# Softmax attention of a hybrid trunk on one core: scores transposed, heads in pairs, maxima ahead

## The chip, the cores and the metric

The kernel runs on one core of a Trainium2 chip. The metric is the device time of one execution in microseconds (us). Three runs of the kernel before took 1719.51, 1723.79 and 1723.97 us, median 1723.79.

## What is computed

Two trunk layers work on 512 latent tokens and, in the first layer, on 256 context tokens with the same weights. Each layer has a modulated norm, one input projection, three groups of heads side by side (mean pooling, gated linear attention, softmax attention), an output projection with a gated residual, and a squared-ReLU MLP. The change is in softmax attention: 8 query heads of 64 in four pairs, 2 key heads (pairs 0 and 1 use the first, 2 and 3 the second). Latent queries see 256 context keys and 512 latent keys in one softmax; context queries see the context keys.

```python
def gqa_attend(qb, k, v):
    s = jnp.einsum('bqhgd,bkhd->bhgqk', qb, k, preferred_element_type=jnp.float32) * HEAD_DIM ** -0.5
    p = jax.nn.softmax(s, axis=-1)
    return jnp.einsum('bhgqk,bkhd->bqhgd', p.astype(v.dtype), v)
...
    o_gl, _, _ = gla_bidir(*gla_features(gq, gk, gv, rf, rb, w_gate, b_gate), s_f, s_b)
...
    mix = jnp.concatenate([pool_mixer(p, w_pool, s_pool),
                           gla_output(o_gl, gg, g_gla, x.dtype),
                           latent_attention(ql, k_all, v_all)], axis=-1) @ w_out
```

In layer 1 the context's outputs aren't needed, only its keys and values, so only the latent queries are swept there.

## The kernel before, in words

Everything is tiled in 128 tokens: latent tiles 0 to 3, context tiles 4 and 5. Matrix products in reduced-precision fp32 keep fp32 precision by splitting each factor in a high and a low part: `wload` (L130 to L146) loads a weight tile into a buffer `raw`, ScalarE rounds it to `whi`, VectorE makes `wlo` as the difference, and a product is three passes (`passes`). `wp` has three buffers for `raw` and five each for "hi" and "lo"; `sp` has 33 slots of 128x768 for everything else in the attention stage. Accumulators are in PSUM: two of 1024 columns (`psA`), three of 512 (`psB`), one of 512 (`psC`).

The instructions of a layer are written by several generators, and the two strings `STEPS` say in what order their steps are written: g for gated linear attention, a for the other projections, m for modulation, t for softmax attention. Within softmax attention, `att_thread` (L1037) calls the pooling generator once per unit. A list scheduler then fixes the order on each engine when the program is built; each engine runs its own list in that order and waits by semaphores.

Softmax attention before. `k_stack` transposes the normalised keys and keeps, for each key head, `kh` (the high part on 64 partitions, twice) and `kl` (the low part, twice). `q_stack` (L1023) does the same for the queries of a pair of heads, with high and low part on top of each other in `qs`, so that one matmul over 128 rows with `kh` and one with `kl` give the exact score. A unit is two query tiles of a pair of heads, and there are 12 in layer 0 (eight latent, four context) and 8 in layer 1. For each of a unit's four score tiles [128 queries x 768 keys], TensorE does four matmuls (L974, L975), VectorE takes the row maximum (L977), and ScalarE does the exponential with the maximum as bias and the row sum as a by-product (L978). `value_part` of the unit before is written between them: per key tile four transposes of probabilities (`pT`, L992), an eviction by ScalarE or VectorE (`pe`, L996, L998), and two value matmuls for 256 queries each (`av`, L1001). At a unit's end the reciprocal sums are spread over 64 partitions by four small matmuls (`rb`, L1008) and multiplied in (L1014), the result is split in `mixh` (ScalarE, L1016) and `mixl` (GpSimd, L1017).

Around it run, on the same engines, the last part of gated linear attention: products `xq`, `xk` on VectorE and GpSimd (L699, L707), small diagonal blocks on TensorE (`att`, L722) copied by VectorE (`dg`, L735) and ScalarE (`AT`, L738), the output `o` (L756, L761), its norm (`ss` L771, `rg` L782), and pooling (`pool`, L920).

The output projection follows (`op`, L291): its weights `w_out` come through `raw` like all others.

## Time and profile before

| | us |
|---|---|
| median of three runs | 1723.79 (1719.51 to 1723.97) |
| span of the profiled execution | 1719.9 |
| TensorE busy | 1639.1 (95%) |
| VectorE busy | 866.9 (50%) |
| ScalarE busy | 656.9 (38%) |
| GpSimd busy | 480.3 (28%) |

The profile shows one execution; its own time is the span, 1719.9 us, and no time outside of it is shown with it. Busy time is the sum of an engine's instructions; TensorE's are pipelined, so the distance between starts says what a matmul costs, not its length. Attention of layer 0 lies between about 222 and 387 us, that of layer 1 between about 1179 and 1305 us. In a row of the timeline the columns are start, length, engine, line, operation, output from inputs, shape and count, with the idle time of the engine before it and what ended that in brackets. The groups give count, busy time, mean ns of one, and the engine's idle time before them.

### The profile page before, as it was taken

How to read it: one execution, taken by the hardware profiler on the slowest of the kernel's cores; microseconds unless marked ns; L12 is line 12 of the kernel's file. 1: busy time of each engine (PE TensorE's matmuls, PEld its weight loads, DVE VectorE, ACT ScalarE, POOL GpSimd, SP SyncE). 2: the span in 40 equal slices, each digit the busy share in tenths (PEclk: the TensorE clock that was granted, in tenths of full speed). 3: DMA queues.
4: the chain of work that ended last, by engine and by line, in shares of the span. 5: the costliest groups of instructions: out<-in, count | busy, mean ns of one | idle time of the engine just before them, and what ended most of it. 6: DMA issues, size and time to landing. Idle time of an engine off the chain costs nothing.

```text
span 1719.9 us, 28685 instructions
## 1 busy us (share of the span) xinstructions
PE 1639.1 (95%) x12059; PEld 1337.3 (78%) x12059; DVE 866.9 (50%) x1209; ACT 656.9 (38%) x1136; POOL 480.3 (28%) x514
## 2 busy tenths in 40 slices
...
GB/s 309 131 85 75 136 161 3 100 27 122 111 138 96 153 50 184 120 94 147 50 122 56 68 89 75 72 2 2 2 74 130 79 99 98 99 98 98 98 98 49
DMA packets 140256, 163.38 MB, mean 95 GB/s; under 512 B 9412, under 2 KB 116304, under 8 KB 140128
## 3 DMA queue, kind: packets, MB, share of 16 engines
...
## 4 chain that ended last, share of the span: by engine, by line
PE 85%; DVE 5%; POOL 3%; DMA 2%; ACT 2%; issue 2%; SPq 0%; ACTq 0%; POOLq 0%; DVEq 0%
PE dn L291 25%; PE up L272 19%; PE op L291 7%; PE tm L291 6%; PE up L274 5%; PE fm L272 4%; PE av L1001 3%; PE pT L992 2%; PE pm L175 2%; PE up L281 2%; PE fm L274 2%; DMA rawm<-in_w_mod_dram 1%; PE sc L974 1%; PE att L722 1%; PE sc L975 1%
## 5 line engine op out<-in xcount | busy, mean ns | idle before, releaser
L144 ACT ACTIVATE whi<-raw 128x1024 fp32r<-128x1024 f32 (+2 forms) x182 | 184.8, 1031 | 582.2 <-PE dn L291 310.3
L1131 POOL TENSOR_TENSOR X<-X,rtmp 128x512 f32<-128x512 f32 x158 | 218.0, 1384 | 660.9 <-DVE rtmp L1130 660.6
L68 DVE TENSOR_TENSOR wlo<-raw,whi 128x1024 fp32r<-128x1024 f32 (+2 forms) x182 | 225.5, 1247 | 279.0 <-ACT whi L144 273.7
L291 PE MATMUL dn<-whi,ah 128*128 128x512 f32 x640 | 249.8, 390 | 0.4 <-DVE rtmp L1130 0.4
L291 PE MATMUL dn<-whi,al 128*128 128x512 f32 x640 | 249.1, 389 | 0.0
L291 PE MATMUL dn<-wlo,ah 128*128 128x512 f32 x640 | 246.8, 389 | 0.0
L1130 DVE TENSOR_TENSOR rtmp<-dn,ga 128x512 f32<-128x512 f32 x160 | 109.2, 689 | 231.4 <-PE dn L291 229.8
L272 PE MATMUL up<-h2h,whi 128*128 128x512 f32 x464 | 183.8, 396 | 0.7 <-ACT relu L1173 0.7
L272 PE MATMUL up<-h2l,whi 128*128 128x512 f32 x464 | 182.5, 393 | 0.0
L272 PE MATMUL up<-h2h,wlo 128*128 128x512 f32 x464 | 182.5, 393 | 0.0
L291 PEld LDWEIGHTS dn<-whi,ah 128*128 128x128 f32 x640 | 120.1, 188 | 29.8 <-ACT whi L144 4.2
L291 PEld LDWEIGHTS dn<-wlo,ah 128*128 128x128 f32 x640 | 120.1, 188 | 25.0
L291 PEld LDWEIGHTS dn<-whi,al 128*128 128x128 f32 x640 | 120.1, 188 | 24.5
L272 PEld LDWEIGHTS up<-h2h,whi 128*128 128x128 f32 x464 | 87.1, 188 | 31.4 <-ACT relu L1173 7.6
L272 PEld LDWEIGHTS up<-h2l,whi 128*128 128x128 f32 x464 | 87.1, 188 | 21.1 <-issue 1.7
L291 PE MATMUL tm<-whi,hTh 128*128 128x256 f32 (+1 forms) x352 | 102.6, 292 | 0.0
L272 PEld LDWEIGHTS up<-h2h,wlo 128*128 128x128 f32 x464 | 87.1, 188 | 19.6
L291 PE MATMUL tm<-whi,hTl 128*128 128x256 f32 (+1 forms) x352 | 101.3, 288 | 0.0
L291 PE MATMUL tm<-wlo,hTh 128*128 128x256 f32 (+1 forms) x352 | 100.5, 287 | 0.0
L291 PE MATMUL op<-whi,mixh 128*128 128x256 f32 x320 | 91.2, 285 | 0.9 <-ACT whi L144 0.9
L291 PE MATMUL op<-wlo,mixh 128*128 128x256 f32 x320 | 90.2, 284 | 0.3 <-DVE wlo L68 0.3
L291 PE MATMUL op<-whi,mixl 128*128 128x256 f32 x320 | 90.5, 283 | 0.0
...
## 6 DMA issues: line engine op xcount, KB each, us to landing
...
```

Source lines behind the costliest of these rows:

```text
L68: V.tensor_tensor(lo, full, hi.bitcast(F32), ALU.subtract)
L144: A.activation(hi, raw, AF.Copy)
L175: T.matmul(pm[32 * j:32 * j + 32, :], sstat[:, k, :], raw[:, (j % 2) * 512:(j % 2) * 512 + 512], start=(k == 0), stop=(k == KT - 1), skip_ ...
L272: T.matmul(ps[:, 0:NL], a, b[:, 0:NL], start=st, stop=sp_)
L274: T.matmul(ps[:, NL:NT], a, b[:, NL:NT], start=st, stop=sp_)
L281: T.matmul(ps[:, cs], a, b[:, cs], start=(k == 0 and i == 0), stop=(k == nk - 1 and i == 2))
L291: T.matmul(ps, a[:, sl], bb, start=(k == 0 and i == 0), stop=(k == nk - 1 and i == 2))
L722: T.matmul(ps[g * bw:(g + 1) * bw, o0:o0 + bw], xk[rows, j0:j0 + bw], xq[rows, i0:i0 + bw], start=True, stop=True)
L992: T.transpose(pt_[:, i * 128:(i + 1) * 128], p_[:, ki * 128:(ki + 1) * 128], ident)
L1001: T.matmul(av_[64 * hh:64 * hh + 64, 0:256], vst, pe[:, hh * 256:hh * 256 + 256], start=(ki == 0), stop=(ki == len(kts) - 1))
L1130: V.tensor_tensor(tmp, ps, ga[0 if t < 4 else 1][:, sl], ALU.mult)
L1131: (V if b == NB - 1 and not both and t == 3 else G).tensor_tensor(X[t][:, sl], X[t][:, sl], tmp, ALU.add)
```

## The change

Scores are computed transposed: 128 keys on the partitions, the 512 latent queries of a head along the columns, the two heads of a pair side by side in 1024 columns. So the exponentials of a key tile (`p`, one 128x1024 instruction) can be used as the moving operand of the value matmuls (`av`, 64x512 per head) without being transposed, and the 416 transposes of probabilities with their evictions are gone.

The maximum of a query is then one value per column, and it goes in by the matmul: `qm` holds the queries' high part on 64 partitions and minus the maximum in a 65th row, and the 65th row of `kl` is ones, written by ScalarE instead of the second copy of the low part that GpSimd made. The maxima must be known before the first score of the pair. `max_part` takes them from separate products, [128 queries x keys] as before but for a latent pair 3 x 512 columns per latent tile (`mxc` for the context keys of both heads, with high and low part of the queries; `mx` per head for the latent keys, high part only), reduced by VectorE (L981, L984) and moved into the 65th row by a matmul with the identity (`mT`, L992) and two ScalarE copies of one row (L995).

The row sum no longer comes with the exponential. GpSimd adds key tiles 0 to 3 (`acc`, L1041, L1043), VectorE tiles 4 and 5 and the two halves (L1049, L1050), in buffers of the pool `raw`; a matmul with ones adds over the partitions (`sum`, L1010). `weigh` takes the reciprocal by ScalarE's logarithm and exponential and one correction step on VectorE (L1013 to L1017), then splits the result as before. `weigh` is put in a list and written two steps later. `max_part` of the next pair is written between the steps of this pair, one step each. The pooling generator is called at every fifth step. Other lines of the diff take out comments and shorten `STEPS`.

```diff
 STEPS = ("aggaamgmagagaaagaaaamgaaaaamagaaaagaaaaaagmgaaaagamggmggmgtt"
-         "mggtttmtttgttgtmgtggtttgtttgttmgtmtgttmgtt",
...
+         "ggttttgtgtgtggttgttgtgtgtgt",
...
+    identr = const.tile([128, 128], F32R, name="identr")
+    V.tensor_copy(identr, ident)
+
+    nmx = const.tile([128, 6, 33], F32R, name="nmx")
+    A.activation(nmx, ident[:, 0:1].unsqueeze(1).to_broadcast([128, 6, 33]), AF.Copy, scale=0.0)
...
-                G.tensor_copy(kl[64:128], kl[0:64].bitcast(F32))
+                A.activation(kl[64:65], ident[64:65, 64:65].to_broadcast([1, NT]), AF.Copy)
...
+        def max_part(hp):
             mix_new(4 + hp)
             pq = [psB("qT"), psB("qT")] if both else [psB("qT")]
             for t in live:
                 T.transpose(pq[t // 4][:, (t % 4) * 128:(t % 4 + 1) * 128], qview(t, hp), ident)
             for hh in range(2):
+                qs, qm = slot("qs", F32R), slot("qm", F32R)
+                hr, lr = slice(64 * hh, 64 * hh + 64), slice(64 - 64 * hh, 128 - 64 * hh)
                 for i, pq_ in enumerate(pq):
                     n0, n1 = (0, NL) if i == 0 else (NL, NT)
+                    src = pq_[hr, 0:n1 - n0]
+                    A.activation(qs[hr, n0:n1], src, AF.Copy)
+                    sub_lo(qs[lr, n0:n1], src, qs[hr, n0:n1])
+                G.tensor_copy(qm[0:64, 0:N_], qs[hr, 0:N_].bitcast(F32))
+                qst[2 * hp + hh] = (qs, qm)
+            yield
+            kh = kst[hp // 2][0]
+            parts = mp.tile([128, 2, 6, 2], F32, tag="mxp", name=nm("mxp"), bufs=1)
+            for t in live:
+                ts_ = slice(t * 128, (t + 1) * 128)
+                ps = psB("mxc")
+                for hh in range(2):
+                    T.matmul(ps[:, hh * NC:(hh + 1) * NC], qst[2 * hp + hh][0][:, ts_], kh[:, NL:NT], start=True, stop=True)
+                if t < 4:
+                    pl_ = [psB("mx"), psB("mx")]
+                    for hh in range(2):
+                        hr = slice(64 * hh, 64 * hh + 64)
+                        T.matmul(pl_[hh], qst[2 * hp + hh][0][hr, ts_], kh[hr, 0:NL], start=True, stop=True)
+                V.tensor_reduce(parts[:, 1, t], ps.rearrange("p (h k) -> p h k", h=2), AX.X, ALU.max, negate=True)
+                if t < 4:
+                    for hh in range(2):
+                        V.tensor_reduce(parts[:, 0, t, hh:hh + 1], pl_[hh], AX.X, ALU.max, negate=True)
+                yield
+            V.tensor_tensor(nmx[:, 0:4, 0:33:32], parts[:, 0, 0:4], parts[:, 1, 0:4], ALU.min)
+            if both:
+                V.tensor_copy(nmx[:, 4:6, 0:33:32], parts[:, 1, 4:6])
+            yield
+            ps = psA("mT")
+            for t in live:
+                T.matmul(ps[0:33, t * 128:(t + 1) * 128], nmx[:, t], identr, start=True, stop=True)
+            for hh in range(2):
+                r0 = 32 * hh
+                A.activation(qst[2 * hp + hh][1][64:65, 0:N_], ps[r0:r0 + 1, 0:N_], AF.Copy)
+            yield
+        def scores(ps, hp, hh, kt, q0, qn):
+            kh, kl = kst[hp // 2]
+            qs, qm = qst[2 * hp + hh]
+            ks = slice(kt * 128, (kt + 1) * 128)
+            T.matmul(ps, kh[:, ks], qs[:, q0:q0 + qn], start=True, stop=False)
+            T.matmul(ps, kl[0:65, ks], qm[0:65, q0:q0 + qn], start=False, stop=True)
+        def weigh(hp, f, acc, q0, n):
+            sm = psB("sum")[:, 0:n]
+            for hh in range(2):
+                T.matmul(sm[64 * hh:64 * hh + 64], one.to_broadcast([128, 64]), acc[hh], start=True, stop=True)
+            r, u = slot("r", w=512)[:, 0:n], slot("u", w=512)[:, 0:n]
+            A.activation(r, sm, AF.Ln)
+            A.activation(r, r, AF.Exp, scale=-1.0)
+            V.scalar_tensor_tensor(u, r, -1.0, sm, ALU.mult, ALU.mult)
+            V.tensor_tensor(r, f, r, ALU.mult)
+            V.scalar_tensor_tensor(r, u, 2.0, r, ALU.add, ALU.mult)
+            mhi, mlo = mixT[4 + hp]
+            A.activation(mhi[:, q0:q0 + n], r, AF.Copy)
+            G.tensor_tensor(mlo[:, q0:q0 + n], r, mhi[:, q0:q0 + n].bitcast(F32), ALU.subtract)
+        def lat_part(hp):
+            av = psC("av")
+            P = []
+            def values(kt):
+                for hh in range(2):
+                    T.matmul(av[64 * hh:64 * hh + 64, :], vview(kt, hp // 2), P[kt][:, hh * 512:hh * 512 + 512],
+                             start=(kt == 0), stop=(kt == 5))
+            for kt in range(6):
+                s_ = psA("sT")
+                for hh in range(2):
+                    scores(s_[:, hh * 512:hh * 512 + 512], hp, hh, kt, 0, NL)
+                P.append(wp.tile([128, 1024], F32, tag="lo" if kt % 2 else "hi", name=nm("p")))
+                A.activation(P[kt], s_, AF.Exp)
+                if kt:
+                    values(kt - 1)
+                if kt == 1:
+                    acc = wp.tile([128, 1024], F32, tag="raw", name=nm("acc"), bufs=3)
+                    G.tensor_tensor(acc, P[0], P[1], ALU.add)
+                elif kt in (2, 3):
+                    G.tensor_tensor(acc, acc, P[kt], ALU.add)
+                yield
+            values(5)
+            acc2 = wp.tile([128, 1024], F32, tag="raw", name=nm("acc"), bufs=3)
+            f = slot("f", w=512)
+            A.activation(f, av, AF.Copy)
+            V.tensor_tensor(acc2, P[4], P[5], ALU.add)
+            V.tensor_tensor(acc, acc, acc2, ALU.add)
+            later.append([2, lambda: weigh(hp, f, [acc[:, 0:512], acc[:, 512:1024]], 0, NL)])
+            yield
+        def ctx_part(hp):
+            av = psC("avc")[:, 0:NC]
+            s_ = psA("sTc")
+            for hh in range(2):
+                for i in range(2):
+                    o = i * 512 + hh * NC
+                    scores(s_[:, o:o + NC], hp, hh, 4 + i, NL, NC)
+            p_ = wp.tile([128, 1024], F32, tag="hi", name=nm("p"))
+            A.activation(p_, s_, AF.Exp)
+            yield
+            for i in range(2):
+                for hh in range(2):
+                    o = i * 512 + hh * NC
+                    T.matmul(av[64 * hh:64 * hh + 64, :], vview(4 + i, hp // 2), p_[:, o:o + NC],
+                             start=(i == 0), stop=(i == 1))
+            f = slot("f", w=512)[:, 0:NC]
+            A.activation(f, av, AF.Copy)
+            acc = slot("accx", w=512)
+            G.tensor_tensor(acc, p_[:, 0:512], p_[:, 512:1024], ALU.add)
+            later.append([2, lambda: weigh(hp, f, [acc[:, 0:NC], acc[:, NC:512]], NL, NC)])
+            yield
+        later = []
+        def tick():
+            for e in list(later):
+                e[0] -= 1
+                if e[0] == 0:
+                    later.remove(e)
+                    e[1]()
         def att_thread():
             k_stack()
             yield
+            yield from max_part(0)
+            n = 0
+            for hp in range(4):
+                nxt = max_part(hp + 1) if hp < 3 else iter(())
+                next(nxt, None)
+                for part in (lat_part(hp), ctx_part(hp) if both else iter(())):
+                    for _ in part:
+                        next(nxt, None)
+                        tick()
+                        n += 1
+                        if n % 5 == 3:
+                            next(pool_, None)
+                        yield
+                for _ in nxt:
+                    tick()
                     yield
             run(pool_)
+            while later:
+                tick()
```

The order on TensorE in layer 0, first inside pair 2 of the kernel before: `sc` are score tiles, `pT` and `av` belong to the unit before.

```order
L1001 MATMUL av_586_4005<-pe_593_4036,UV_185_1137 64x256 x2
L992 MATMUL pT_600_4072<-ident_86,p_558_3910 128x128
L992 MATMUL pT_600_4072<-ident_86,p_559_3911 128x128
L992 MATMUL pT_600_4072<-ident_86,p_560_3912 128x128
L992 MATMUL pT_600_4072<-ident_86,p_561_3913 128x128
L974 MATMUL sc_599_4065<-kh_350_2665,qs_490_3634 128x512
L975 MATMUL sc_599_4065<-kl_351_2666,qs_490_3634 128x512
L974 MATMUL sc_599_4065<-kh_350_2665,qs_490_3634 128x256
L975 MATMUL sc_599_4065<-kl_351_2666,qs_490_3634 128x256
L1001 MATMUL av_586_4005<-pe_595_4045,UV_185_1137 64x256 x2
L1008 MATMUL rb_602_4082<-ident_86,sm_556_3908 64x128 x4
L1001 MATMUL av_586_4005<-pe_598_4061,UV_185_1137 64x256 x2
```

The same engine now, from the end of pair 1's value matmuls on: `mxc` and `mx` are the products for pair 2's maxima, `pool` is pooling, `sum_496` sums pair 0's context part.

```order
L1028 MATMUL av_489_3625<-p_519_3730,UV_185_1141 64x512 x2
L1028 MATMUL av_489_3625<-p_522_3743,UV_185_1141 64x512 x2
L975 MATMUL mxc_493_3634<-kh_350_2669,qs_485_3611 128x256
L927 MATMUL pool_517_3719<-pm_291_2163,wpl_138_743 128x256
L975 MATMUL mxc_493_3634<-kh_350_2669,qs_487_3618 128x256
L980 MATMUL mx_494_3637<-kh_350_2669,qs_485_3611 128x512
L980 MATMUL mx_495_3638<-kh_350_2669,qs_487_3618 128x512
L1010 MATMUL sum_496_3644<-accx_480_3599,one_97 64x256 x2
L975 MATMUL mxc_502_3667<-kh_350_2669,qs_485_3611 128x256
L975 MATMUL mxc_502_3667<-kh_350_2669,qs_487_3618 128x256
L980 MATMUL mx_503_3670<-kh_350_2669,qs_485_3611 128x512
L980 MATMUL mx_504_3671<-kh_350_2669,qs_487_3618 128x512
```

Score tiles stood between the transposes and value matmuls of the unit before; now the products for the next pair's maxima stand behind the last value matmul of the pair.

VectorE in layer 0 before, in pair 2: `nmx` are row maxima, `qs` the low part of the next queries, `pe` evictions.

```order
L977 TENSOR_REDUCE nmx_557_3909<-sc_572_3964 128x1
L68 TENSOR_TENSOR qs_578_3987<-qT_575_3974,qs_578_3987 64x512
L977 TENSOR_REDUCE nmx_580_3993<-sc_585_3998 128x1
L68 TENSOR_TENSOR qs_578_3987<-qT_576_3975,qs_578_3987 64x256
L980 RECIPROCAL sm_556_3908<-sm_556_3908 128x4
L977 TENSOR_REDUCE nmx_580_3993<-sc_591_4024 128x1
L998 COPY pe_593_4036<-pT_592_4031 128x512
L977 TENSOR_REDUCE nmx_580_3993<-sc_596_4049 128x1
L998 COPY pe_601_4077<-pT_600_4072 128x512
L977 TENSOR_REDUCE nmx_580_3993<-sc_599_4065 128x1
```

VectorE now, at the end of pair 2's scores: `acc_581` adds the exponentials of its last two key tiles, `mxp` are the maxima of pair 3, `pm` is pooling.

```order
L68 TENSOR_TENSOR qs_544_3834<-qT_540_3819,qs_544_3834 64x512
L68 TENSOR_TENSOR qs_544_3834<-qT_541_3820,qs_544_3834 64x256
L1049 TENSOR_TENSOR acc_581_3977<-p_573_3938,p_579_3967 128x1024
L981 TENSOR_REDUCE mxp_549_3849<-mxc_550_3850 128x2
L984 TENSOR_REDUCE mxp_549_3849<-mx_551_3853 128x1
L984 TENSOR_REDUCE mxp_549_3849<-mx_552_3854 128x1
L920 SCALAR_TENSOR_TENSOR pm_296_2220<-pl_536_3802,invw_121,pl_535_3801 64x512
L920 SCALAR_TENSOR_TENSOR pm_296_2220<-pl_537_3803,invw_121,pl_535_3801 64x512
L981 TENSOR_REDUCE mxp_549_3849<-mxc_559_3883 128x2
L984 TENSOR_REDUCE mxp_549_3849<-mx_560_3886 128x1
```

Each score tile's maximum stood in the list on its own, with the next tile's; now all of a pair's reductions come together, behind the addition of the pair before.

TensorE now where pair 1's first scores begin: `mT` moves the maxima, `rg` belongs to linear attention, `sum_473` adds up pair 0's latent exponentials.

```order
L992 MATMUL mT_472_3558<-identr_91,nmx_93 33x128 x6
L1003 MATMUL sT_490_3626<-qs_411_3143,kh_348_2663 128x512
L787 MATMUL rg_463_3514<-ident_86,rsg_460_3505 64x128 x8
L787 MATMUL rg_464_3525<-ident_86,rsg_460_3505 64x128 x4
L1010 MATMUL sum_473_3567<-acc_427_3246,one_97 64x512 x2
L1004 MATMUL sT_490_3626<-qm_412_3144,kl_349_2664 128x512
L1003 MATMUL sT_490_3626<-qs_413_3150,kh_348_2663 128x512
L1004 MATMUL sT_490_3626<-qm_414_3151,kl_349_2664 128x512
L1003 MATMUL sT_499_3656<-qs_411_3143,kh_348_2663 128x512
```

The first score matmul of pair 1 (`sT_490`) stands ahead of `rg` and of pair 0's sum, the other three behind them.

TensorE now at the end of layer 0's attention; `op` is the output projection.

```order
L1028 MATMUL av_592_4025<-p_611_4098,UV_185_1141 64x512 x2
L1067 MATMUL avc_614_4109<-p_616_4119,UV_185_1141 64x256 x4
L1010 MATMUL sum_617_4121<-acc_603_4062,one_97 64x512 x2
L296 MATMUL op_648_4348<-whi_643_4338,mixh_515_3717 128x256
L296 MATMUL op_648_4348<-whi_643_4338,mixl_516_3718 128x256
L296 MATMUL op_649_4349<-whi_643_4338,mixh_515_3717 128x256
L296 MATMUL op_649_4349<-whi_643_4338,mixl_516_3718 128x256
```

The last matmul ahead of the projection is the sum of pair 3, which reads `acc_603`; the projection starts with `whi_643`, its third loaded tile.

98 lines of the change are left out of this document (2 added, 96 removed).

## The prediction

> **What bounds the kernel now.** I read the page first, for the busiest engine, and its chain of waits.
>
> ```profile
> span 1719.9 us, 28685 instructions
> PE 1639.1 (95%) x12059; PEld 1337.3 (78%) x12059; DVE 866.9 (50%) x1209; ACT 656.9 (38%) x1136; POOL 480.3 (28%) x514
> PE 85%; DVE 5%; POOL 3%; DMA 2%; ACT 2%; issue 2%; SPq 0%; ACTq 0%; POOLq 0%; DVEq 0%
> ```
>
> TensorE is busy for 95% of the span and makes 85% of the chain, so a TensorE microsecond saved is mostly a microsecond of time, as long as nothing else becomes late. That average doesn't speak for the attention stage. The stretches of the two attention stages come next (layer 0 in the first two rows, layer 1 in the last three; after length: busy time of PE, PEld, DVE, ACT, POOL, then granted clock).
>
> ```profile
> core 0: us, PE busy (x) PEld busy (x) DVE busy (x) ACT busy (x) POOL busy (x), PEclk, DMA share, GB/s
> 247.87:297.90 50.03, 41.53 (x938) 30.05 (x938) 43.04 (x59) 36.46 (x80) 29.11 (x37) 0.90 0.03 8
> 297.90:386.71 88.81, 82.34 (x633) 55.52 (x626) 49.45 (x83) 56.99 (x135) 14.82 (x23) 0.98 0.17 61
> 1179.40:1215.00 35.60, 28.97 (x405) 20.25 (x402) 29.35 (x44) 27.11 (x59) 23.93 (x35) 0.86 0.01 2
> 1215.00:1255.00 40.00, 34.41 (x478) 22.63 (x479) 26.73 (x51) 21.49 (x49) 8.15 (x14) 0.96 0.01 2
> 1255.00:1307.00 52.00, 50.78 (x380) 35.17 (x377) 29.71 (x42) 36.17 (x72) 6.75 (x7) 1.00 0.35 123
> ```
>
> Each stage has two halves. In the front one, which gated linear attention shares, VectorE is as full as TensorE (43.04 against 41.53 us of 50). In the back one TensorE is the bound (82.34 of 88.81; 50.78 of 52) and VectorE has half its time free. So VectorE work that lies beside matmuls is free in the back half, and VectorE work that TensorE must wait for isn't.
>
> **TensorE's price for a pair of heads.** Starts of successive pieces, from the timeline of TensorE in layer 0:
>
> ```profile
> start us, us, engine line op out<-in xcount [idle before <-releaser]
> 313.23 0.50 PE L974 MATMUL sc<-kh,qs 128*128 128x512 f32 x1
> ...
> 314.05 0.40 PE L974 MATMUL sc<-kh,qs 128*128 128x512 f32 x1
> ...
> 314.84 1.53 PE L782 MATMUL rg<-ident,rsg 128*64 128x128 f32 x24
> ...
> 320.58 0.65 PE L1001 MATMUL av<-pe,UV 128*64 128x256 f32 x4
> 321.06 0.61 PE L1008 MATMUL rb<-ident,sm 128*64 128x128 f32 x8
> 321.60 1.12 PE L920 MATMUL pool<-pm,wpl 128*128 128x512 f32 x2
> 322.66 0.65 PE L1001 MATMUL av<-pe,UV 128*64 128x256 f32 x4
> 323.24 0.66 PE L992 MATMUL pT<-ident,p 128*128 128x128 f32 x4
> ...
> 324.41 1.53 PE L992 MATMUL pT<-ident,p 128*128 128x128 f32 x12
> 325.87 1.08 PE L1001 MATMUL av<-pe,UV 128*64 128x256 f32 x8
> 326.88 0.66 PE L992 MATMUL pT<-ident,p 128*128 128x128 f32 x4
> ...
> 386.71 0.38 PE L291 MATMUL op<-whi,mixh 128*128 128x256 f32 x1 [0.90 <-ACT whi L144]
> ```
>
> A score piece (four matmuls for 128 queries of one head) takes 0.82 us, from 313.23 to 314.05. Four transposes take 0.49 us (1.46 for twelve) when they come in a row; one key tile's value step takes 0.51 us in a row (1.01 for two) and 0.58 alone (322.66 to 323.24). The reciprocal broadcast takes 0.54 us.
> Before, a latent pair of heads costs 8 score pieces (6.5), 12 sets of transposes (5.9), 12 value steps (6.5) and two broadcasts (1.1): 20.0 us.
> After, each of the six key tiles has a score step of four 512-column matmuls and a value step for 512 queries. The score step has 2048 columns where the 0.82 piece has 1536, so 1.0 us with its start; the value step is twice the old, so 1.0: 12.0 in all. The maxima's own matmuls are 4 x 1024 + 4 x 512 columns, 2.7 us at the same price per column; the maxima's transposes (six of 128) take 0.7 and the matmul that sums takes 1.0 (like a value step). Together 16.4 us. The context part has the same eight score matmuls of 256 columns and changes by a few tenths, left out. TensorE is relieved of 3.6 us a pair, 29 us for eight pairs. I take that as certain work; the question is whether TensorE stays the bound.
>
> **The other engines' prices.** Groups by form (count, busy time, mean ns):
>
> ```profile
> L977 DVE TENSOR_REDUCE nmx<-sc 128x1 f32<-128x768 f32 x64 | 60.5, 953 | 25.9 <-PE sc L975 25.5
> L962 DVE TENSOR_REDUCE nmx<-scc 128x4 f32<-128x1024 f32 x4 | 4.9, 1223 | 2.0 <-PE scc L961 1.9
> L699 DVE TENSOR_TENSOR xq<-xq,gq 128x768 f32<-128x768 f32 x14 | 16.8, 1209 | 0.8 <-ACT xq L698 0.7
> L1175 DVE TENSOR_TENSOR relu<-relu 128x768 f32<-128x768 f32 x32 | 30.5, 954 | 58.9 <-ACT relu L1173 58.9
> L978 ACT ACTIVATE p<-sc,nmx 128x768 f32<-128x768 f32 x64 | 57.5, 899 | 18.7 <-DVE nmx L977 18.1
> L996 ACT ACTIVATE pe<-pT 128x512 f32<-128x512 f32 x72 | 41.5, 597 | 22.3 <-PE pT L992 18.4 <-PE av L1001 3.4
> L1131 POOL TENSOR_TENSOR X<-X,rtmp 128x512 f32<-128x512 f32 x158 | 218.0, 1384 | 660.9 <-DVE rtmp L1130 660.6
> ```
>
> A maximum over 512 columns is 0.68 us on the line through 953 ns at 768 and 1223 at 1024. A pair in layer 0 has 14 of them (three for each of four latent tiles, one for each of two context tiles): 9.5 us. Layer 1 has 12: 8.2 us. Before, a pair had 8 x 0.95 + 1.2 = 8.8 us in layer 0, so the amount hardly changes. What changes is when it is needed: the old score piece was followed by its own maximum while TensorE did the previous unit's transposes and values; the new exponentials can't begin until all maxima of the pair are done, transposed and copied into the 65th row.
>
> The 1024-column exponential is 1.1 us by the line through 0.90 at 768 and the 0.60 of a 512-column copy, six for a pair, which fits beside the 2.0 us of a key tile. ScalarE's 72 evictions of transposes (41.5 us) go, and VectorE's with them; they were beside TensorE's work, so that frees room and ends no wait. GpSimd gets three 1024-column additions a pair, at twice 1.38 us each 8.3 us; bounds are 5 us (half its span taken as rough) and 10. In 28 us there is room, but the sum waits for the third addition and then for VectorE's two.
>
> Here the products of gated linear attention run beside GpSimd: 1209 ns against 954 for the same form without it (xq against relu). The Trainium skill, "SBUF — State Buffer", section "Who interferes with whom", has it that a VectorE instruction with two SBUF inputs contends with a GpSimd instruction that reads SBUF, and that a reduce never does. By that rule the new additions would slow the products and acc steps, not the maxima; the two rows agree, and at 27% on six such steps a pair it would be 1 to 2 us, inside the range below.
>
> **Where the maxima come now.** In the order of layer 0, the maxima of the next pair stand behind this pair's scores on TensorE: six value steps of pair 1 in a row, then the matmuls of pair 2's maxima, then the sum. On VectorE pair 3's reductions stand behind `acc_581_3977`, the addition of pair 2's last two key tiles, which can't run until pair 2's sixth exponential is done. So the maxima have nothing of size to hide behind, and TensorE has 2.7 us of matmuls in some 11 us.
>
> Layer 0 step by step. Until the first pair's scores can start, VectorE has 14 maxima (9.5) and 11 products of the old queue at 1.2 (13) and some small steps (2): 25 us from 247.9, then the row copies, so 275. From there TensorE has some 30 us to do (six score and value steps 12, the next pair's maxima 2.7, diagonal blocks 5, output of linear attention 7, the small rest 3) and about 7 us of waits, for the products that both kernels wait for. That brings `rg` to 312; it stood at 314.84, so the front half ends 3 us early. What follows:
> - Pair 1: scores at one exponential each 6.4, context 1.0, value steps behind them 6.0, maxima 9.5 and the three small weighting steps among them 1.3, then what stands ahead of the next exponent on ScalarE (the sum 1.0, logarithm and exponential 0.6 each, two row copies of 768 at 0.8) 3.8; rg 1.5, the first sum 1.0, pooling 1.6, transposes of queries 0.6. That is 32.7.
> - Pair 2: scores and values 12.0, context 1.5, maxima 9.5, small steps 1.3, the chain 3.8: 28.1.
> - Pair 3, which has no maxima behind it: 12.0, 1.5, pooling 1.6, sums 1.5: 16.6.
>
> Sum 77.4, so 389.4, against 386.71 now: the output projection would be 2.7 us late on these alone.
>
> It is later still by a load. The chain of waits at the end of the stage:
>
> ```profile
> 381.82 3.76 DMA raw<-in_w_out_dram
> 385.58 0.02 issue
> 385.60 1.06 ACT whi L144
> ...
> 386.69 1.24 DVE wlo L68
> ```
>
> Now the load of `w_out` goes out at 381.82, once an eviction's buffer is free, and TensorE waits 0.90. The two sums of exponentials now hold buffers of the same three-deep pool until the matmul that sums has read them, which is TensorE's last one in the stage, and the first matmuls of the projection use the third loaded tile. 3.76 + 1.06 + 0.2 = 5.0 us then lie open where 0.9 do. Bounds: 0.9 (the tile lands in a buffer that was free early) and 6.3 (the low part's 1.24 us on VectorE too). I take 5. Layer 0: 394.4 against 386.7, so 8 us slower.
>
> Layer 1, whose projection begins here:
>
> ```profile
> 1242.34 0.44 PE L756 MATMUL o<-AT,GU 128*64 128x128 f32 x4
> 1302.11 0.39 PE L291 MATMUL op<-whi,mixh 128*128 128x256 f32 x1
> ```
>
> Pair 0's maxima and pair 1's both lie beside linear attention, as the old ones did; pair 2's first two tiles lie beside pair 1's scores and the other two behind. I put pair 1's start at 1240.6, a little ahead of where `o` starts now, since the new order has it behind pair 0's values and nothing of attention behind it: the 12 reductions and 10 products before the first exponent end at about 1206, and 34 us of TensorE and product work follow. Then 12.0 + 4.1 (six maxima) + 2.1 + 3.8 + pooling, rg and ss 2.5 = 24.5; 12.0 + 4.1 + 2.1 + 3.8 = 22.0; 15.0 for the last. That is 1302.1, no change.
>
> The profiled execution spans 1719.9 us, 3.9 under the median of 1723.79. 1719.9 + 8 + 1 for the contention = 1728.9, and the median moves alike: 1733. A change under 0.3%, 5.2 us, is about what a measurement of this kernel can't tell from none.
>
> **The rivals.**
> - *The relief arrives in the front halves* (0.25), faster. The first pair's maxima and products are what I let TensorE wait for. But the stretch is also freed: ahead of the last diagonal block of layer 0 VectorE has 26 new maxima (17.7 us), 12 old ones fewer (11.7) and some 9 us of evictions, query and pooling steps fewer, so 3 us less in all, and TensorE has 10 us less up to there. If the two keep each other busy, `rg` starts at 302 and not 312, layer 1's second pair likewise 10 us sooner, and with the load hidden (4 us) it is 8 − 4 − 10 − 10 = −16: 1708. For it: VectorE is 43.04 of 50 busy there now, so the rest of the 50 is waiting that could go. Against: the first scores can't start until VectorE has done 25 us of work in its order, and they started at once before. It decides where `rg` of layer 0 starts: before 305 this case, after 310 mine.
> - *Level* (0.18): half of that, so that layer 1 gains the 4 to 8 us that layer 0 loses, 1720 to 1728.
> - *The change doesn't put off what it says* (part of the forecast): `sum_473_3567` stands between the first and second matmul of pair 1's first score step, so a late GpSimd addition stops the scores it was to hide behind. 2 to 3 us at two places.
> - *The clock falls in the maxima* (0.15). In the front half TensorE was once nearly idle:
>
> ```profile
> 269.70:273.10 3.40, 1.00 (x14) 0.60 (x6) 2.93 (x5) 1.05 (x2) 3.40 (x5) 0.89 0.00 0
> 273.10:276.50 3.40, 2.52 (x65) 1.22 (x64) 3.37 (x5) 2.61 (x5) 1.74 (x4) 0.50 0.03 7
> 276.50:279.90 3.40, 3.40 (x97) 2.60 (x94) 3.34 (x7) 1.36 (x3) 1.27 (x3) 0.61 0.02 5
> ```
>
> One window with TensorE busy for 1.00 of 3.40 us was followed by about 5 us at half clock. The new maxima have 2.7 us of matmuls in 11, a like share. Five us at half clock cost about 2.5 us; with six such phases in two layers that is 15 us on top of the 8: 1747. Against: the maxima's matmuls come every 0.7 us, not in one lump. The Trainium skill, "TensorE: Matmul & The Clock Gate", section "HAM oscillation — how this bites in real kernels", says to let TensorE have no idle gap over about 3.4 us. By that rule alone the spread maxima would keep the clock, since no gap among them is that long; the row above is a window with some work in it that lost the clock all the same, so I don't rest on the rule.
>
> **How the numbers follow.** Forecast 0.42 (1733; 1728 to 1740 by the bounds of the load and of GpSimd), relief 0.25, level 0.18, clock 0.15. Slower by over 0.3%: 0.42 + 0.15 = 0.57. Same: 0.18. Faster: 0.25. The range reaches down to 1703, 5 us below the relief case, and up to 1750 to take in the clock case as priced; what lies outside are the tails of these two.
>
> **What would show it.** Right: in layer 0 TensorE busy for under a third between pair 1's last value step and pair 2's first exponential, 10 us or more there; `op` first at 392 or later, its idle released by the load; layer 1's `op` within 3 us of 1302. Wrong: `rg` of layer 0 before 305 and `op` before 385; no open load there; reductions of pair 2 that run while pair 1's value steps do; or a 512-column maximum well under 0.68 us.

## The result and the profile after

The changed kernel takes 1775.18 us (median of 4 runs, 1774.44 to 1778.28) beside 1723.88 for the kernel before on the same chip: a ratio of 1.031 (95% interval 1.0291 to 1.0328). It is slower by 51 us, where 9 were forecast. The profiled execution took 1775.29 us, with a span of 1773.2. From its page, the totals, the granted clock in 40 slices and the shares of the chain:

```profile
span 1773.2 us, 27374 instructions
PE 1662.5 (94%) x11459; PEld 1311.7 (74%) x11459; DVE 906.3 (51%) x1238; ACT 631.0 (36%) x985; POOL 552.2 (31%) x546
PEclk9999885889999999999999999898799999999999
PE 82%; DVE 7%; POOL 3%; ACT 3%; DMA 2%; issue 2%; SPq 0%; ACTq 0%; POOLq 0%; DVEq 0%
```

There are 600 matmuls fewer, and yet TensorE is busy for 23 us longer: the seventh slice (266 to 310 us, layer 0's attention) was granted half to six tenths of the clock. The two attention stages as windows, from the transposes of the keys (`kT`) to the first `op` of each layer, in the kernel after and then in the one before (after the length: busy PE, PEld, DVE, ACT, POOL, granted clock, DMA share, GB/s):

```profile
222.00:419.60 197.60, 159.19 (x1441) 82.76 (x1439) 128.63 (x194) 88.33 (x138) 92.83 (x90) 0.81 0.17 60
1214.90:1352.10 137.20, 115.50 (x936) 58.60 (x934) 94.74 (x136) 67.79 (x109) 70.77 (x69) 0.80 0.08 28
```

```profile
222.40:386.70 164.30, 146.99 (x1757) 97.40 (x1754) 105.09 (x174) 102.77 (x230) 55.29 (x74) 0.96 0.18 66
1179.50:1302.10 122.60, 109.17 (x1219) 73.58 (x1216) 82.62 (x131) 82.17 (x175) 38.83 (x55) 0.94 0.12 44
```

Of the 53.3 us that the span grew, 33.3 lie in the first stage and 14.6 in the second; the rest is a few us in the long stretches between, which vary by as much from kernel to kernel. Each stage can be split into three: TensorE idle (length less busy), clock loss (TensorE's busy time times one less the granted clock, summed here over windows of 2 us), and what is left, the work at full clock.

| stage | kernel | length | idle | clock loss | work at full clock |
|---|---|---|---|---|---|
| layer 0 | before | 164.3 | 17.3 | 6.1 | 140.8 |
| layer 0 | after | 197.6 | 38.4 | 29.4 | 129.8 |
| layer 1 | before | 122.6 | 13.4 | 5.4 | 103.8 |
| layer 1 | after | 137.2 | 21.7 | 21.6 | 93.8 |

So the change did relieve TensorE, by 21 us of work. It lost 29 us to idle time and 39.5 to the clock. The split comes from one execution of each kernel.

**Where the clock went.** Windows of the kernel after in layer 0: the last at full clock, the stretch at half clock in two parts, and the first at full clock again.

```profile
247.39:250.80 3.41, 2.01 (x38) 1.24 (x38) 3.41 (x6) 3.41 (x6) 0.22 (x1) 1.00 0.30 77
250.80:281.50 30.70, 20.04 (x537) 13.61 (x528) 27.77 (x37) 17.18 (x31) 22.29 (x20) 0.50 0.01 3
281.50:302.00 20.50, 20.50 (x170) 9.54 (x172) 10.38 (x18) 3.08 (x3) 8.46 (x10) 0.50 0.00 1
302.00:305.40 3.40, 3.40 (x90) 2.06 (x75) 1.77 (x6) 1.74 (x5) 0.00 (x0) 0.98 0.02 5
```

TensorE ran at half clock for 51 us, and for the last 20 of them it was busy all the time. No idle gap keeps it there. The window that lost the clock was busy for 2.01 of 3.41 us. A window as full, of the kernel before, kept it:

```profile
265.57:268.98 3.41, 1.97 (x12) 1.29 (x12) 3.18 (x5) 3.39 (x7) 3.41 (x3) 1.00 0.03 5
```

What differs is what ran: in the second, matmuls over all 128 rows (scores, transposes, values); in the first, mostly the 64-row matmuls of the latent maxima and the small `att` of linear attention. The 20 busy us at half clock hold the new scores, of which every other matmul uses 65 rows, more of the 64-row ones, and some full ones. That made a theory that the experiments test.

**Where the idle time went.** Layer 0's path, from TensorE's timeline (start, duration, what ended the idle time): the end of the front half, pair 1's six value steps, the start of pairs 2 and 3, the output projection.

```profile
318.32 1.53 PE L787 MATMUL rg<-ident,rsg 128*64 128x128 f32 x24
...
338.94 7.41 PE L1028 MATMUL av<-p,UV 128*64 128x512 f32 x24 [1.39 <-ACT f L1070]
...
360.46 0.48 PE L992 MATMUL mT<-identr,nmx 128*33 128x128 f32 x4
...
393.36 0.64 PE L992 MATMUL mT<-identr,nmx 128*33 128x128 f32 x4
...
419.60 0.58 PE L296 MATMUL op<-whi,mixh 128*128 128x256 f32 x1 [4.86 <-ACT whi L149]
```

And one of its stalls, from the timeline of all engines:

```profile
328.17 5.12 POOL L1043 TENSOR_TENSOR acc<-acc,p 128x1024 f32<-128x1024 f32 x2
...
328.85 2.24 DVE L1016 TENSOR_TENSOR r<-f,r 128x512 f32<-128x512 f32 x1
...
331.13 2.72 DVE L1017 SCALAR_TENSOR_TENSOR r<-u,r 128x512 f32<-128x512 f32 x1
...
333.88 0.63 ACT L1019 ACTIVATE mixh<-r 128x512 fp32r<-128x512 f32 x1 [3.79 <-DVE r L1017]
334.42 1.01 ACT L1036 ACTIVATE p<-sT 128x1024 f32<-128x1024 f32 x1
...
335.47 0.58 PE L1003 MATMUL sTc<-qs,kh 128*128 128x256 f32 x1 [4.13 <-ACT p L1036]
```

Read this from the bottom. TensorE waits 4.1 us for an exponential. That stands in ScalarE's queue behind `mixh`, which waits 3.8 us for the two weighting steps of the pair before, and those take 2.24 and 2.72 us while GpSimd adds. The put-off weighting stops the scores that it was to lie behind.

A score step and the value step behind it in pair 3, where the clock was full, and the stretch from pair 1's last value step to pair 2's first exponential as a window:

```profile
398.01 0.50 PE L1003 MATMUL sT<-qs,kh 128*128 128x512 f32 x1
...
399.14 1.08 PE L1028 MATMUL av<-p,UV 128*64 128x512 f32 x4
400.15 0.50 PE L1003 MATMUL sT<-qs,kh 128*128 128x512 f32 x1
```

```profile
346.35:364.24 17.89, 13.67 (x57) 7.10 (x58) 14.22 (x23) 5.90 (x10) 2.54 (x2) 0.90 0.00 1
```

The groups of five operations in the kernel after (count, busy, mean ns):

```profile
L1036 ACT ACTIVATE p<-sT 128x1024 f32<-128x1024 f32 x48 | 48.9, 1024 | 53.2 <-PE sT L1004 52.6
L984 DVE TENSOR_REDUCE mxp<-mx 128x1 f32<-128x512 f32 x64 | 42.5, 682 | 7.9 <-PE mx L980 7.7
L1016 DVE TENSOR_TENSOR r<-f,r 128x512 f32<-128x512 f32 x8 | 7.1, 889 | 0.2
L1017 DVE SCALAR_TENSOR_TENSOR r<-u,r 128x512 f32<-128x512 f32 x8 | 7.5, 944 | 0.2
L1043 POOL TENSOR_TENSOR acc<-acc,p 128x1024 f32<-128x1024 f32 x16 | 39.8, 2490 | 11.0 <-ACT p L1036 10.6
```

### The profile page after: what moved, and what is told of

Its sections match the earlier page's. It is cut to its first block, busy times and chain, and to the rows that moved or that the text cites. A ratio compares the mean times of both kernels' runs of the same rounds, so it can differ in the third digit from the quotient of the medians.

```text
span 1773.2 us, 27374 instructions
## 1 busy us (share of the span) xinstructions
PE 1662.5 (94%) x11459; PEld 1311.7 (74%) x11459; DVE 906.3 (51%) x1238; ACT 631.0 (36%) x985; POOL 552.2 (31%) x546
## 3 DMA queue, kind: packets, MB, share of 16 engines
q1 hardware_dynamic: 133312, 147.10, 26.2%
## 4 chain that ended last, share of the span: by engine, by line
PE 82%; DVE 7%; POOL 3%; ACT 3%; DMA 2%; issue 2%; SPq 0%; ACTq 0%; POOLq 0%; DVEq 0%
PE dn L296 24%; PE up L277 18%; PE op L296 6%; PE tm L296 6%; PE up L279 5%; PE fm L277 4%; PE pm L180 2%; PE up L286 2%; PE av L1028 2%; PE fm L279 1%; PE sT L1003 1%; PE sT L1004 1%; PE att L727 1%; DVE mxp L984 1%; DMA rawm<-in_w_mod_dram 1%
## 5 line engine op out<-in xcount | busy, mean ns | idle before, releaser
L277 PEld LDWEIGHTS up<-h2h,wlo 128*128 128x128 f32 x464 | 87.1, 188 | 19.5
```

The costliest lines, as they stand in the source:

```text
L277: T.matmul(ps[:, 0:NL], a, b[:, 0:NL], start=st, stop=sp_)
```

## The experiments

Two theories. **Rows** (R in the expectations): matmuls that use 64 or 65 of the 128 rows hold the clock less than full ones, so the change's new matmuls lose it and don't get it back. **Stacked waits** (S): the maxima on VectorE, the additions on GpSimd and the early weighting lie on one path, so that taking away one uncovers the next. The rivals were a single dominant cause (the maxima, the additions, the load at the stage's end or the order of the steps) and a clock that only follows idle time. The expectations name them by letters too: V for VectorE's maxima, G for GpSimd's additions, L for the load, O for the order, and C and B for a clock that follows busy time. Times are medians, ratios are to the kernel before on the same chip (about 1722 us each time), and "idle" and "clock loss" are those of the table above. Differences are shown against the kernel after, unless said otherwise; `...` marks lines left out.

One caution holds for all of them: the list scheduler sorts each version anew. By the order of the traces, between 40 (the maxima alone over all rows) and 700 (the old step strings) of TensorE's 11,459 matmuls stand at another place than in the kernel after, beside what the edit itself changes. No run takes away one step and leaves all else as it was, and differences of a few us between two versions can come from the order.

### Single causes

**The maxima's matmuls three times** (they rewrite the same values): does filling the wait hold the clock?

```diff
+REP = 3
...
-                for hh in range(2):
+                for hh in (0, 1) * REP:
...
-                    for hh in range(2):
+                    for hh in (0, 1) * REP:
```

> The changed kernel with each matmul that makes a product for the maxima issued three times into the same place (nothing else changes; the last one counts). Theory C (the clock): while the maxima are made, TensorE has so little to do that the granted clock falls to a half (252 to 302 us and 1224 to 1261 us after the change), and most of the 51 us is work done at that clock. Then more work brings it back: mean clock 0.97 or more, 1750 to 1762 us in place of 1775. Theory V (VectorE): TensorE waits for the row of reductions, whatever its clock. Then the clock may recover, but the time stays within 8 us of 1775 or grows by the 5 us a pair of added matmuls.

Measured: 1789.28 us, ratio 1.0391 (1.0373 to 1.0409). The stages got 41 us more work, 12 us less idle time and 14 us less clock loss (37.2 against 51.0), 15 more in all. So part of the clock loss follows from idle time, but filling it costs more than it gives. The theory of the clock alone, which asked for 1750 to 1762 us, failed.

**Short reductions** (the maxima are taken over 64 of 512 columns, and the exponentials are of zero):

```diff
-                V.tensor_reduce(parts[:, 1, t], ps.rearrange("p (h k) -> p h k", h=2), AX.X, ALU.max, negate=True)
+                V.tensor_reduce(parts[:, 1, t], ps.rearrange("p (h k) -> p h k", h=2)[:, :, 0:32], AX.X, ALU.max, negate=True)
...
-                        V.tensor_reduce(parts[:, 0, t, hh:hh + 1], pl_[hh], AX.X, ALU.max, negate=True)
+                        V.tensor_reduce(parts[:, 0, t, hh:hh + 1], pl_[hh][:, 0:64], AX.X, ALU.max, negate=True)
...
-                A.activation(P[kt], s_, AF.Exp)
+                A.activation(P[kt], s_, AF.Exp, scale=0.0)
```

> The changed kernel with each reduction of the maxima reading only 64 columns of its 512 (instruction count, matmuls and waits stay; the maxima are then those of a part of the keys, and the exponentials' scale is zero so that they stay finite). A reduction should take about 0.15 us in place of 0.68, so 104 of them 55 us less of VectorE. Theory V: the time falls by 30 us or more, to 1745 or less, since the phases between pairs shrink by some 7 us each. Theory C gives a like fall if the phases become short enough for the clock to stay; what tells them apart is the run with more matmuls. If neither holds and GpSimd's additions set the pace, it falls by under 15 us.

Measured: 1769.58 us, 1.0271 (1.0249 to 1.0293). The groups of reductions in this kernel:

```profile
L984 DVE TENSOR_REDUCE mxp<-mx 128x1 f32<-128x64 f32 x64 | 13.3, 220 | 15.6 <-PE mx L980 15.3
L981 DVE TENSOR_REDUCE mxp<-mxc 128x2 f32<-128x64 f32 x40 | 8.8, 220 | 23.6 <-PE mxc L975 23.2
```

104 reductions went from 682 to 220 ns, 48 us of VectorE's time, and the median fell by 6, where the theory of the maxima asked for 30. The maxima alone are not the cause.

**No additions on GpSimd** (the sums of exponentials leave out three of six key tiles, and the exponentials are of zero):

```diff
-                    G.tensor_tensor(acc, P[0], P[1], ALU.add)
-                elif kt in (2, 3):
-                    G.tensor_tensor(acc, acc, P[kt], ALU.add)
...
-            V.tensor_tensor(acc, acc, acc2, ALU.add)
+            V.tensor_tensor(acc, P[3], acc2, ALU.add)
```

> The changed kernel without GpSimd's three additions per pair (the sums leave out the first three key tiles; the exponentials' scale is zero so that they stay finite). Theory G: the additions hold up VectorE's steps with two inputs beside them (two of 512 columns took 2.24 and 2.72 us at 329 to 334 us, where 0.69 is usual) and the sums come late; 8 to 15 us less than 1775 then, and these steps at 0.7 us. If V or C is all there is, under 4 us.

Measured: 1774.93 us, 1.0305 (1.0285 to 1.0326). The weighting steps in this kernel:

```profile
L1017 DVE SCALAR_TENSOR_TENSOR r<-u,r 128x512 f32<-128x512 f32 x8 | 5.5, 690 | 0.2
L1016 DVE TENSOR_TENSOR r<-f,r 128x512 f32<-128x512 f32 x8 | 5.5, 688 | 0.2
```

They lose their stretch beside GpSimd, layer 0 has 7 us less idle time, and its clock loss grows by 9. The time stays, where 8 to 15 us less was expected if the additions alone were the cause.

**The sums in place**, so that no buffer of the weight loads is held:

```diff
-                    acc = wp.tile([128, 1024], F32, tag="raw", name=nm("acc"), bufs=3)
+                    acc = P[0]
...
-            acc2 = wp.tile([128, 1024], F32, tag="raw", name=nm("acc"), bufs=3)
+            acc2 = P[4]
```

> The changed kernel with the sums of exponentials made in place, in the first and fifth key tile's buffers, so that the three buffers of the weight loads stay free. Theory L: the 4.9 us that TensorE waits for the first weights of the output projection in layer 0 go, and about 2 us in layer 1; 1768 to 1770 us. If the buffers weren't what the load waited for, 1775 stays and the idle time at the projection too.

Measured: 1773.13 us, 1.0297 (1.0279 to 1.0315). The wait of 4.86 us ahead of `op` is gone (it starts at 416.78 there). The median is 2 us lower, which the overlapping intervals can't tell from none.

**The step strings of before**, that is the old interleaving of the steps of linear attention, modulation and softmax attention in both layers:

```diff
-         "ggttttgtgtgtggttgttgtgtgtgt",
-         "ggggagaggaaagaaggaaaaaagaaaagaaaggaagaagga"
-         "ttgtttgtgtgttgggttgtggtttgttgt")
+         "mggtttmtttgttgtmgtggtttgtttgttmgtmtgttmgtt",
+         "ggggagaggaaagaaggaaaaaagaaaagaaaggaagaaggatatgatttttgaatgttg"
+         "tttgggtttgttggttttgtttgt")
```

> The changed kernel with the step strings of the kernel before (more steps of linear attention ahead of the end of softmax attention; in the resulting lists the maxima of pair 1 stand between its predecessor's scores). Theory O: a list with the maxima beside scores is faster, 1755 to 1768. Theory S or C: 1770 or more, since the first pair's maxima stay as sparse as they are, and the strings were made for the other kernel.

Measured: 1771.47 us, 1.0292 (1.0265 to 1.0319). The interval overlaps that of the change: the old interleaving can't be told from the new one. Pooling is still called at every fifth step in this kernel, so this is no test of that.

### The rows

**All rows** in the second score matmul, with zeros in the rows that were not used, and in the latent maxima, which take both halves of the queries:

```diff
-                A.activation(kl[64:65], ident[64:65, 64:65].to_broadcast([1, NT]), AF.Copy)
+                A.activation(kl[64:128], ident[64:128, 64:65].to_broadcast([64, NT]), AF.Copy)
...
+                A.activation(qm[64:128, 0:N_], ident[64:128, 0:1].to_broadcast([64, N_]), AF.Copy)
...
-                        T.matmul(pl_[hh], qst[2 * hp + hh][0][hr, ts_], kh[hr, 0:NL], start=True, stop=True)
+                        T.matmul(pl_[hh], qst[2 * hp + hh][0][:, ts_], kh[:, 0:NL], start=True, stop=True)
...
-            T.matmul(ps, kl[0:65, ks], qm[0:65, q0:q0 + qn], start=False, stop=True)
+            T.matmul(ps, kl[:, ks], qm[:, q0:q0 + qn], start=False, stop=True)
```

> The changed kernel with 128 rows in every score and maximum matmul: the second score matmul runs over rows 65 to 127 as well, which hold zeros, and the maxima's latent products take both halves of the queries. Columns, count and length of the matmuls stay; ScalarE gets one more small step per head. Theory R (rows): what holds the clock is how many rows of the array work, not how long TensorE is busy; the stretch from 281 to 302 us was 100% busy and stayed at half clock, and half of its score matmuls use 65 rows and all latent maxima 64. Then the mean clock rises to 0.965 or more, the clock's loss in the two attention stages (29 and 22 us after, 6 and 5 before) falls by 20 us or more, and the time to 1750 to 1760 us. Rival B (busy time only): clock and time as they are, 1770 to 1780.

**Only the maxima** over all rows (the two lines of that difference with `pl_[hh]`):

> The changed kernel with 128 rows in the maxima's latent products alone. R: the clock falls later or less often where the maxima are made; a gain of 5 to 12 us. B: 1770 to 1780.

**Only the second score matmul** over all rows (the other lines):

> The changed kernel with 128 rows in the second score matmul alone. R: the half clock ends sooner once scores run, 270 to 285 us in place of 302; a gain of 8 to 15 us. B: 1770 to 1780.

**All rows and the sums in place** (the differences of both):

> All rows as in the first of these runs, and the sums of exponentials in place so that the weight buffers stay free. R with the load theory: 3 to 6 us below the first of these runs, 1745 to 1756. B: 1770 to 1776.

Measured, in this order: 1772.82 us (1.0288, 1.0269 to 1.0308), 1776.23 (1.0307, 1.0285 to 1.0329), 1772.21 (1.0283, 1.0262 to 1.0304), 1772.17 (1.029, 1.0271 to 1.0309). The theory of the rows had expected 1750 to 1760 us of the first, 5 to 15 us of gain from the next two and 1745 to 1756 us of the last, and 20 us or more off the clock loss; as a forecast of size it missed. The half clock of layer 0 in the kernel with only the scores over all rows, as windows:

```profile
252.00:279.00 27.00, 16.97 (x458) 12.06 (x459) 26.91 (x33) 16.45 (x30) 22.93 (x19) 0.50 0.01 2
279.00:282.40 3.40, 3.40 (x102) 2.20 (x101) 1.25 (x4) 3.01 (x5) 1.01 (x2) 0.50 0.02 5
282.40:285.80 3.40, 3.40 (x12) 1.68 (x13) 3.34 (x7) 1.02 (x1) 1.27 (x4) 0.98 0.00 0
```

The same first score step and the same `att` and `mxc` after it fill one window of 3.4 us, and the clock is back at 282.4; with 65 rows it took 20.5 us of unbroken matmuls, to 302. (There the first score step lies across the end of a window, but six whole windows behind it, all busy, ran at half clock too.) The clock loss of both stages falls from 51.0 to 38.0, and to 48.6 with the maxima alone over all rows. The granted clock of whole executions agrees: 0.955 to 0.958 in the four with all rows, 0.946 to 0.951 in the four of the kernel after. But the idle time grows from 60.1 to 64.3, and the medians fall by 2 to 3 us at most, within overlapping intervals: what TensorE does sooner, it then waits for.

All traces together say the same. In each of them the granted clock changes only at steps of 3.41 us, so each window of that length can be set beside the clock of the next. Count a matmul for 0.235 us per 512 columns at full clock and twice that at half (from the starts in the timelines), times the share of the 128 rows that it uses; this is an estimate, with a limit fitted to each direction. The window that lost the clock above counts for 0.28 of its length, the one that kept it for 0.41. Over all nineteen traces, a limit of 0.375 misjudges 81 of 8905 windows at full clock (316 lost it), and one of 0.83 misjudges 93 of 784 at half clock (297 ended with it back). Busy time without the rows does no better than 124 and 147.

**The kernel before, with 64 rows** in its second score matmul (part of the product of the rounding remainders is left out). Against the kernel before:

```diff
-                        T.matmul(sc_[:, z0:z0 + zn], lq, kl[:, z0:z0 + zn], start=False, stop=True)
+                        T.matmul(sc_[:, z0:z0 + zn], lq[0:64], kl[0:64, z0:z0 + zn], start=False, stop=True)
...
```

> The kernel before the change, with the second matmul of each score over 64 rows in place of 128 (the product of the two low parts is left out). Theory R (rows hold the clock): the reverse of the all-rows runs; half clocks of one window become longer, the clock's loss in the two attention stages rises from 11.5 to 15 us or more, and the time by 2 to 8 us. Rival B: clock and time as before, within 2 us of 1722.

Measured: 1779.37 us, 1.0347 (1.0321 to 1.0374). It is no test of the rows, since something else came with it. TensorE's timeline of one score piece:

```profile
299.80 0.51 PE L974 MATMUL sc<-kh,qs 128*128 128x512 f32 x1
300.24 0.49 PE L975 MATMUL sc<-kl,qs 64*128 64x512 f32 x1
300.66 0.38 PE L974 MATMUL sc<-kh,qs 128*128 128x256 f32 x1
300.98 0.38 PE L975 MATMUL sc<-kl,qs 64*128 64x256 f32 x1
301.29 0.66 PE L1008 MATMUL rb<-ident,sm 128*64 128x128 f32 x8
```

The piece takes 1.49 us (299.80 to 301.29) where it took 0.82. Each change between 128 and 64 rows costs about 0.2 us, and the work of layer 0 at full clock rose from 140.8 to 164.1 us.

**The same with 65 rows** (the same part is left out, but for one row):

```diff
-                        T.matmul(sc_[:, z0:z0 + zn], lq, kl[:, z0:z0 + zn], start=False, stop=True)
+                        T.matmul(sc_[:, z0:z0 + zn], lq[0:65], kl[0:65, z0:z0 + zn], start=False, stop=True)
...
```

> The kernel before with the second matmul of each score over 65 rows in place of 128 (most of the product of the two low parts is left out). The run with 64 rows mixed two things: 64- and 128-row matmuls in turn cost 0.2 us more at each change. With 65 rows the matmuls should take 0.23 and 0.12 us as they do with 128. Theory R: the clock's loss in the two attention stages rises from 11.5 to 15 us or more and the time by 2 to 8 us. Rival B: clock and time within 2 us of 1722.

Measured: 1728.74 us, 1.0041 (1.0027 to 1.0054). A score piece in TensorE's timeline, and the two stages as windows:

```profile
317.74 0.50 PE L974 MATMUL sc<-kh,qs 128*128 128x512 f32 x1
318.07 0.40 PE L975 MATMUL sc<-kl,qs 65*128 65x512 f32 x1
318.31 0.28 PE L974 MATMUL sc<-kh,qs 128*128 128x256 f32 x1
318.43 0.29 PE L975 MATMUL sc<-kl,qs 65*128 65x256 f32 x1
318.55 0.39 PE L974 MATMUL sc<-kh,qs 128*128 128x512 f32 x1
```

```profile
220.90:394.20 173.30, 154.49 (x1758) 102.03 (x1754) 105.51 (x174) 103.01 (x230) 54.10 (x74) 0.90 0.19 64
1186.10:1308.30 122.20, 109.82 (x1220) 74.71 (x1218) 81.05 (x131) 81.88 (x175) 35.73 (x55) 0.94 0.13 44
```

This is the better test of the rows. The piece takes 0.81 us as before, and the work is the same (140.4 and 103.6 us against 140.8 and 103.8). The clock loss rises from 11.5 to 20.3 us, nearly all of it in layer 0, and the time by 0.27 to 0.54%; the granted clock was 0.973 to 0.978 in six executions, against 0.980 to 0.984 in nine of the kernel before. It isn't clean: 159 of 12,059 matmuls stand elsewhere than before, most of them in layer 0's attention, and the longest half clock (13.65 us from 270.59) lies in that stretch, so a part of the rise may be the order's. The lists of all engines are the same as in the kernel with 64 rows, so the cost of 64 rows beside 65 is clean: 1779.37 against 1728.74 us. Both directions and the count over all traces agree with the theory of the rows. It explains a part of the 39.5 us, not the whole: padding the rows of the scores took 11 to 14 away beside full reductions (51.0 to 37.3 and 38.0, and 54.7 to 43.7 with the sums in place), and 24 beside short ones (54.8 to 30.7).

### The waits, taken away together

Each of these has the scores and maxima over all rows.

**All rows and short reductions** (the differences of both; it leaves out what the second kernel above left out):

> All rows (as in the fifth run) and short reductions (as in the second) together; the maxima are those of a part of the keys and the exponentials' scale is zero. Alone these gave 2 and 6 us. Theory S (stacked waits): behind the slow clock lies VectorE's row, and the reverse, so that each alone uncovers the other; together 20 us or more, 1755 or less. Theory O (order): the lists themselves (a pair's scores, then its values, then the next pair's maxima) keep TensorE waiting for chains of short steps whatever one step costs; then the two only add up, 1763 to 1770.

**These and no additions on GpSimd** (it leaves out what the second and the third kernel left out):

> All rows, short reductions and no additions on GpSimd together (the sums leave out three key tiles). S: 1748 or less, since with VectorE's row, the contention and the slow clock gone only TensorE's work is left (20 us less of it than before the change, by the attention stages' accounts). O: 1760 or more.

**All rows, and the latent part weighted 5 steps later instead of 2:**

```diff
-            later.append([2, lambda: weigh(hp, f, [acc[:, 0:512], acc[:, 512:1024]], 0, NL)])
+            later.append([5, lambda: weigh(hp, f, [acc[:, 0:512], acc[:, 512:1024]], 0, NL)])
```

> All rows, and the weighting of a pair's latent part written five steps later in place of two, so that the sum no longer stands between pair 1's first score matmuls and the exponentials no longer queue behind the weighting's last step on ScalarE (TensorE waited 4.1 us there). If that wait is real time, 4 to 8 us below the 1773 of all rows alone; if something else ends last at once, within 3 us.

**The same with the sums in place** (the difference of the sums in place added):

> All computed, nothing left out: all rows, the weighting five steps later, and the sums in place. Theory S (stacked waits) with the load: 4 to 8 us below the 1761 of the run without the sums in place, 1753 to 1758, since the projection's load is no longer behind the last sum. Theory O or a slower list: 1758 or more.

**All rows, short reductions, no additions on GpSimd, weighted later** (all four differences):

> All rows, short reductions, no additions on GpSimd (sums leave out three key tiles) and the weighting five steps later. S: most of what keeps it above the kernel before is then the order of the first pair and the clock there; 1722 to 1730, against 1736 without the later weighting. If the later weighting only helped because of GpSimd's additions: 1734 or more.

**That with full reductions** (the additions are left out still):

> All rows, the weighting five steps later and no additions on GpSimd (sums leave out three key tiles), with full reductions: beside the run with short reductions (1722) it prices the reductions alone. By the prediction's step (VectorE's 0.46 us more for each of 104 reductions lies open) it is 40 us or more slower, 1762; if half of them are hidden, 1735 to 1750.

Measured:

| all rows, and | us | ratio (95%) | idle, both stages | clock loss | 
|---|---|---|---|---|
| nothing else | 1772.82 | 1.0288 (1.0269 to 1.0308) | 68.2 | 37.3 |
| short reductions | 1747.12 | 1.0154 (1.0129 to 1.0178) | 58.3 | 30.7 |
| short, no GpSimd | 1736.20 | 1.0086 (1.0066 to 1.0106) | 51.0 | 24.3 |
| short, no GpSimd, later | 1721.96 | 0.9995 (0.9986 to 1.0005) | 40.5 | 18.1 |
| no GpSimd, later | 1741.42 | 1.0109 (1.0087 to 1.0130) | 52.7 | 26.2 |
| later | 1761.47 | 1.0234 (1.0209 to 1.0258) | 59.4 | 44.8 |
| later, in place | 1770.73 | 1.0287 (1.0268 to 1.0306) | 62.6 | 46.7 |

The stages of the kernel with all four, as windows:

```profile
225.50:389.90 164.40, 141.76 (x1447) 76.46 (x1443) 96.16 (x189) 92.29 (x144) 64.57 (x79) 0.91 0.19 67
1184.30:1300.80 116.50, 98.55 (x935) 54.29 (x933) 66.05 (x136) 71.43 (x119) 38.71 (x57) 0.93 0.10 37
```

Alone, the rows gave 2.4 us, the short reductions 5.6 and the missing additions 0.3: 8 in all. Together they gave 39 (1775.18 to 1736.20), and 53 with the later weighting. In company each is worth far more than alone: the rows 22.5 us beside short reductions (1769.58 to 1747.12), the missing additions 10.9 beside those two, the later weighting 14.2 beside all three. That is what stacked waits look like, and in these steps idle time and clock loss fall together. The later weighting without the others lowers the idle time (68.2 to 59.4) and raises the clock loss (37.3 to 44.8). The expectations of S held for the rows with short reductions, for these without the additions, and for all four. With VectorE's reductions three times as fast, the additions gone and the weighting later, the kernel is level with the one before. Put the full reductions back and it is 19.5 us slower, 40% of the 48 us that they take on VectorE.

The later weighting gave 11 us with everything computed (1772.82 to 1761.47), the best of the versions that leave nothing out; the stall of 4.13 us shown above goes with it (`sTc` starts at 337.93 there, straight behind a value step). In the profiles layer 0's stage became 9.8 us shorter (197.1 to 187.3), layer 1's 8.1 longer (130.0 to 138.1), and the other 6 us of the two spans' difference lie outside the stages. The profiled execution was the slowest of its four (1765.9). With the sums in place the later weighting gave only 1.4 us (1772.17 to 1770.73), where 1753 to 1758 had been expected, though its stages are within 1.1 us of those not in place (187.1 and 139.4): the 9 us between these two kernels don't come from attention as profiled. So the later weighting goes with a shorter layer 0, and its 11 us as a whole are not explained. None of these versions beats the kernel before.

## Why the prediction was right in sign and wrong in size

The step that failed is the sum for the two attention stages: 8 us more in layer 0 and none in layer 1. It took TensorE's work at full clock throughout, and the steps of the other engines as hidden or paid once. The stages grew by 33.3 and 14.6 us instead: 21 us of work less, 29 us of idle time more and 39.5 us of clock loss more. In layer 0, `op` came 25 us after the 394.4 of the sum. With the pairs counted from the starts of `mT`, the rows shown split these 25: the front half 6.3, pair 1 9.4, pair 2 4.8 and pair 3 4.8 us.

- **TensorE's relief, 29 us.** 21 came, as work at full clock. The mechanism was right, the price some 1.0 us a pair too good. Most of that is the score step: put at 1.0 us, where the price of the 0.82 piece gives 1.09 for 2048 columns; it took 1.13 (398.01 to 399.14), 6 us over 48 steps. The value step took the 1.0 us that it was given (399.14 to 400.15).
- **Prices of the other engines.** A maximum over 512 columns 0.68 us: 0.682. A GpSimd addition 2.77: 2.49. An exponential was put at 1.1 us; the line through its two points gives 1.2, and it took 1.02. VectorE's two-input steps beside GpSimd were given 27%, 1 to 2 us in all; at the place shown 0.69 became 2.24 and 2.72, while the maxima kept 0.682. The Trainium skill, "SBUF — State Buffer", section "Who interferes with whom", has the two-input steps contend and the reduces not: the trace agrees on both. The mean stretch was near what was put (889 and 944 ns against 690), but the term was mis-sized, because the one step on the path was stretched three- to fourfold.
- **The front half to 312.** It ended at 318.3. VectorE's serial start was right, but TensorE's "30 us to do" was priced at full clock, and it ran at half clock from 250.8 to 302, where the sum had put no clock term.
- **The pairs, 32.7, 28.1 and 16.6 us.** Measured from the rows above: pair 1 42.1 (318.32 to 360.46), pair 2 32.9 (to 393.36), pair 3 21.4 (to the wait at 414.74). `op` came at 419.6 and not at 394.4. The largest miss lies in the first part of pair 1: 20.6 us to the first value step, where 12.1 were summed, with the stall of 4.13 behind the early weighting in it. The six value steps took 7.4 us for 6.0, and from there to pair 2's first exponential it was 17.9 us, where 9.5, 1.3 and 3.8 were summed.
- **The load, 5.0 us.** It was 4.86, by the releaser named. Without it the median was 2 us lower, no more than the intervals can tell from none.
- **Layer 1, no change.** It was 14.6 us longer, with 16 us of clock loss more and 8 of idle time: nothing in my sum for it was a clock term. This step failed outright: `op` started at 1352.1 and not within 3 us of 1302.
- **The clock rival, 1747.** This was the right mechanism at the wrong size, 15 us where 39.5 came. Its step that failed: a dip costs "about 5 us at half clock", read from one place of the kernel before. The three rows shown there add up to 6.8 us already ((0.11 + 0.50 + 0.39) x 3.4 / 0.5). There the full-row matmuls brought the clock back within one or two windows; with the new ones of 64 and 65 rows it took 51 us in layer 0.
- **The rule of no gap over 3.4 us.** I didn't rest on it, and it would have failed: the window from 247.39 has no such gap and lost the clock. The Trainium skill, "TensorE: Matmul & The Clock Gate", section "What's actually happening", has a busy window of about 3.4 us bring the clock back. With all rows the trace agrees (3.40 busy us from 279.0, then 0.98); with 65 rows it does not (20.50 busy us at 0.50).
- **The change that doesn't put off what it says.** 2 to 3 us at two places was the forecast, by a late sum in TensorE's list. The stall shown above is of 4.13 us and by another way, through ScalarE's queue; with all rows in use, layer 0's stage was 9.8 us shorter with the weighting later.
- **The relief rival, 1708.** It was to be decided by `rg` before 305. It came at 318.3.
- **The signs.** `op` at 392 or later with its idle time released by the load held. TensorE under a third busy between pair 1's last value step and pair 2's first exponential did not: it was busy for 13.67 of 17.89 us (the window above).

What stays open: what exactly the clock gate counts (rows times time fits best, with limits that are fitted and still misjudge some windows); how much of each difference is the new order of the lists, which no run holds fixed against the kernel after; why later weighting lengthens layer 1's stage, and what outside the stages makes 9 us between the sums in place and not in place with it; and what the level kernel still waits for: its stages have 22.5 us less TensorE work than those before, but 9.8 more idle time and 6.6 more clock loss, so that they are 6 us shorter and the time is the same.
